# An encoder layer on one core: long attention tiles and the unit matrix at 32 bytes over a multiple of 128

## The chip, the core and the metric

The kernel runs on one core of a Trainium2 chip (trn2). The metric is the device time of one execution in microseconds: 2098.08 us in the median of 3 runs (2094.0 to 2100.1).

## What is computed

One post-norm layer over a sequence of 2048 rows of 1024 columns, float32, modulated by a conditioning vector. The input projection feeds two mixers. Mixer A takes trailing-window means over 2, 4, 8 and 16 frames in four channel groups. Mixer B is chunked attention with 8 heads of 64, in which each chunk of 64 rows looks at itself and the 8 chunks before.

```
mod = silu(c) @ w_ada + b_ada;  sh1, sc1, g1, sh2, sc2, g2 = split(mod)
h = x * (1 + sc1) + sh1
u, q, k, v = split(h @ w_in)
y_pool[g] = (window_sum(u[g], w[g]) / count - u[g]) @ w_pool[g] * pool_scale
y_attn = softmax(q @ k_band.T / 8 + bias, masked) @ v_band
x = layer_norm(2**0.25 * x + (1 + g1) * (concat(y_pool, y_attn) @ w_out))
h = x * (1 + sc2) + sh2
out = layer_norm(2**0.25 * x + (1 + g2) * (square(relu(h @ w_ff1)) @ w_ff2))
```

## The kernel before

All products of the projections are split: each float32 operand becomes a high part in fp32r and a low part (what is left), and three fp32r products (high by high, high by low, low by high) take the place of one float32 product. `split` (L58) makes the parts: ScalarE copies the high part, VectorE or GpSimd subtracts (L59, L60). The `Stream` (L62) loads weights into the two buffers `raw` and splits them into the three buffers `hl`.

The program is written in the order in which its engines run it; nothing is scheduled behind it (`manual_schedule`). It has four parts, one after the other:

1. The input projection with the attention beside it. `dense` (L421) goes through the heads and groups of output columns; each step issues 24 products of 128x512 (L446) into a PSUM bank, from the stationary weights `hl` and the moving rows `hT`. Between them the loop at the end of this part takes 128 units, each a block of 128 queries of one head: `scores` (L617) multiplies `q` by `k` (L628), VectorE adds the bias and takes the extreme value into the score tile `s` (L635), ScalarE exponentiates in place (L637), GpSimd divides in place (`normalise`, L640, at L643). Then `transposes` (L645) turns each 128x128 block of `s` on TensorE with the unit matrix `ident` as the moving operand (L651), `probs` splits it into `PT` (L659, L660), `values` multiplies by `v` (L672), and `combine` adds the halves into `y` through `yl` (L683, L684). The values `vt` are transposed with `ident` as well (L343).
2. The output projection (L407) and the first layer norm. The normalised rows `n` are transposed with `ident` (L844).
3. The first feed-forward product (L1070), in blocks of a 2 by 2 scheme with 7 products instead of 8.
4. The second feed-forward product (L1354), stationary `sa`, moving `sb`, and the second layer norm in `stats` and `ln2` (from L1314).

Mixer A is in `evac` (L316), in the branch from L350: `u` holds a halo of 16 columns that GpSimd copies from the block before, and 512 columns that ScalarE copies from PSUM; GpSimd then doubles the window in 1 to 4 sums between `ws0` and `ws1` (L361), VectorE subtracts (L370), and a DMA stores the result. `extras` (L498) sums the conditioning products in between, from tiles `xr` into `xa` (L514), and folds the pool weights `wp` into the output weights (L561).

Memory is given out by pools, in the order of the code. `const` and `small` hold what lives throughout, `stream` the buffers `raw` and `hl`; `ap` is the pool of the attention part, and the pools of the later parts take its place when it is closed. `padr` and `big` (the tiles `hT`, later `sb` and `g`) stand at the far end. Two fillers, `padr` (L118) and `pad` (L151), shift what follows them.

Of the kernel before, what the change touches and what calls it, by code (L numbers as in the profile page):

```python
# [8 lines left out]
F32 = mybir.dt.float32  # L9
F32R = mybir.dt.float32r  # L10
AF = mybir.ActivationFunctionType
ALU = mybir.AluOpType
# [12 lines left out]
def trunk_layer(ctx: ExitStack, tc: tile.TileContext, xT, x, wada1, wada2, vecs, rows, win, wfirst, wpT, wout,  # L25
# [2 lines left out]
    PS, DR = bass.MemoryType.PSUM, bass.MemoryType.DRAM  # L28
    ctx.enter_context(tc.manual_schedule())
    const = ctx.enter_context(tc.tile_pool(name="const", bufs=1))  # L30
    stream = ctx.enter_context(tc.tile_pool(name="stream", bufs=1))
    dram = ctx.enter_context(tc.tile_pool(name="scratch", bufs=1, space=DR))

    yS = [dram.tile([8, 128, 8, 128], F32, name=f"yS{i}") for i in range(2)]
# [8 lines left out]
    wS = [dram.tile([2, 128, 1024], F32, name=f"wS{i}") for i in range(16)]  # L43
    xS = [dram.tile([1024, 1024], F32, name=f"xS{i}") for i in range(2)]

    ident = const.tile([128, 128], F32, name="ident")
    make_identity(nc, ident)
    ones = const.tile([128, 1], F32, name="ones")
# [4 lines left out]
    nc.sync.dma_start(vec, vecs)  # L53
    mod1 = const.tile([128, 8, 2], F32, name="mod1")
    mods = const.tile([128, 2, 8], F32, name="mods")
    small = ctx.enter_context(tc.tile_pool(name="small", bufs=2))

    def split(hl_h, hl_l, src, low):  # L58
# [66 lines left out]


    e = small.tile([128, 8], F32, name="e")
    cs = const.tile([128, 8], F32, name="cs")
    nc.scalar.activation(e, vec[:, V_C:V_C + 8], AF.Exp, scale=-1.0)
    nc.vector.tensor_scalar(e, e, 1.0, None, op0=ALU.add)  # L130
    nc.vector.reciprocal(e, e)
# [184 lines left out]
    def evac(hf, kind, idx, tb, ps, bank):  # L316
        cols = slice(tb * 512, tb * 512 + 512)
        if kind == "A":
            q, kk = Qt[hf, idx], Kt[hf, idx]
            kc = slice(512 + tb * 512, 1024 + tb * 512)  # L320
            nc.scalar.activation(q[0:64, cols], ps[0:64], AF.Copy, scale=-0.125)
            nc.scalar.copy(kk[64:128, 0, kc], ps[64:128])
            yield
            nc.vector.scalar_tensor_tensor(q[64:128, cols], ps[0:64], -0.125, q[0:64, cols].bitcast(F32),
                                           op0=ALU.mult, op1=ALU.subtract)
            yield
            nc.vector.tensor_sub(kk[64:128, 1, kc], ps[64:128], kk[64:128, 0, kc].bitcast(F32))

            def copy():
                nc.sync.dma_start(kk[0:64, :, kc].bitcast(F32), kk[64:128, :, kc].bitcast(F32))  # L330
                if hf == 0 and tb == 1:
                    nc.sync.dma_start(kS[idx].bitcast(F32), kk[64:128, :, kc].bitcast(F32))

            after(12, copy)
        elif kind == "V":
            vv = Vt[hf, idx]
            vt = ap.tile([128, 512], F32, name="vt", bufs=1)
            nc.scalar.copy(vt, ps)  # L338
            for _ in range(9):
                yield  # L340
            pt = bank()
            for j in range(4):
                nc.tensor.transpose(pt[:, j * 128:j * 128 + 128], vt[:, j * 128:j * 128 + 128], ident)  # L343
            o = vv[:, 4 + tb * 4:8 + tb * 4]
            src = pt.rearrange("p (j h d) -> p j h d", j=4, h=2)
            nc.scalar.copy(o[:, :, :, 0:64], src)
            nc.vector.tensor_sub(o[:, :, :, 64:128], src, o[:, :, :, 0:64].bitcast(F32))
            if hf == 0 and tb == 1:
                after(12, lambda: nc.sync.dma_start(vS[idx].bitcast(F32), o.bitcast(F32)))
        else:  # L350
            wd = WINDOWS[idx]
            flush()
            u = ap.tile([128, 528], F32, name="u", bufs=1)
            nc.scalar.copy(u[:, 16:528], ps)
            nc.gpsimd.tensor_copy(u[:, 0:16], uh[:, idx, :])
            nc.gpsimd.tensor_copy(uh[:, idx, :], u[:, 512:528])
            ws = [ap.tile([128, 528], F32, name=f"ws{i}", bufs=1) for i in range(2)]
            cur, lo, sh, i = u, 0, 1, 0
            while sh < wd:
                lo += sh  # L360
                nc.gpsimd.tensor_add(ws[i][:, lo:528], cur[:, lo:528], cur[:, lo - sh:528 - sh])  # L361
                cur, i, sh = ws[i], 1 - i, 2 * sh
                for _ in range(3):
                    yield
            pl = ws[i][:, 16:528]
            for _ in range((30 if (hf, idx) == (0, 0) else 18) - 3 * (idx + 1)):
                yield
            if hf == 0 and tb == 0:
                nc.vector.tensor_mul(cur[:, 16:32], cur[:, 16:32], vec[:, V_CNT + 16 * idx:V_CNT + 16 * idx + 16])
            nc.vector.scalar_tensor_tensor(pl, cur[:, 16:528], 1.0 / wd, u[:, 16:528], op0=ALU.mult,  # L370
                                           op1=ALU.subtract)
            after(12, lambda: nc.sync.dma_start(
                yS[hf][tb * 4:tb * 4 + 4, :, idx, :].rearrange("t p c -> p t c"),
                pl.rearrange("p (t c) -> p t c", t=4)))
# [408 lines left out]

    load_x(0)
    load_x(1)
    a2 = const.tile([128, 8], F32, name="a2")
    b2 = const.tile([128, 8], F32, name="b2")
    nc.vector.tensor_mul(a2, vec[:, V_G:V_G + 8], mods[:, 1, :])
    nc.vector.tensor_mul(b2, vec[:, V_B:V_B + 8], mods[:, 1, :])
    nc.vector.tensor_add(b2, b2, mods[:, 0, :])  # L790
# [522 lines left out]

    def stats(t, halves=(0, 1)):  # L1314
        if t not in lns:
            lns[t] = (f2l.tile([128, 2, 6], F32, name="z6", bufs=5), f2l.tile([128, 4], F32, name="zv", bufs=5), [])
        s6, mv, got = lns[t]
        for i in halves:
            nc.vector.bn_stats(s6[:, i, :], acc[t][:, i * 512:i * 512 + 512])
# [149 lines left out]
```

## Time and profile before

| | |
|---|---|
| median of 3 runs | 2098.08 us |
| lowest and highest | 2094.0 and 2100.1 us |
| the profiled execution | 2097.0 us |
| its span, first to last instruction | 2095.3 us |
| granted TensorE clock, mean | 0.993 |
| TensorE busy with products | 2026.7 us, 97% |
| VectorE, ScalarE, GpSimd busy | 1311.3, 1000.4 and 323.1 us |
| moved by DMA | 456.68 MB, 218 GB/s |

Busy time is the time in which an engine works on an instruction; the weight loads of TensorE (PEld) overlap its products (PE). A matmul's own duration holds the way through the array, so that products that follow each other overlap in the rows: the pace of a series is the distance between the starts.

### The profile page before, as it was taken

The page shows a single profiled execution, that of the slowest core. Times are in us where ns is not written, and L with a number is a line of the kernel's source. Part 1 is how long each engine was busy: PE and PEld are TensorE (multiplying, and loading weights), DVE is VectorE, ACT ScalarE, POOL GpSimd, SP SyncE. Part 2 cuts the span into 40 slices and gives each one's busy share as a digit, 9 for nine tenths or more (in the row PEclk, how much of TensorE's full clock was granted, in tenths as well). Part 3 has the DMA queues.
Part 4 walks back from the last instruction along what each step waited for, and adds up shares of the span by engine and source line. Part 5 has one row for each costly group of instructions (what it writes and reads, how often), then busy time and mean ns, then how long its engine had stood idle before and what let it go on. Part 6 is the DMA issues. An engine that isn't in the chain of part 4 may idle for free.

```text
span 2095.3 us, 27047 instructions
## 1 busy us (share of the span) xinstructions
PE 2026.7 (97%) x9672; PEld 1682.5 (80%) x9672; DVE 1311.3 (63%) x1974; ACT 1000.4 (48%) x1592; POOL 323.1 (15%) x427
## 2 busy tenths in 40 slices
PE   7999989999999999899999999999999999999998
PEld 6788878887877888678888788888788888888886
DVE  7555566556665464777776766666594547875448
ACT  5544456555544545545555655545453333333330
POOL 1535443544233100000000000000000001000002
PEclk9999999999999999999999999999999999999999
DMA  7444543444443678879878988888886566776552
GB/s 299 137 136 135 144 148 103 132 119 141 130 128 100 190 252 285 297 262 321 289 275 300 313 281 307 295 295 284 318 290 219 190 199 211 248 239 234 193 171 110
DMA packets 210360, 456.68 MB, mean 218 GB/s; under 512 B 18609, under 2 KB 36529, under 8 KB 209202
## 3 DMA queue, kind: packets, MB, share of 16 engines
q1 hardware_dynamic: 210226, 454.96, 64.8%
q8 instruction: 76, 1.25, 0.3%
q14 instruction: 58, 0.48, 0.1%
HBM read 294.45 MB, written 152.05 MB: 213 GB/s over the span
## 4 chain that ended last, share of the span: by engine, by line
PE 80%; DVE 8%; ACT 4%; DMA 3%; issue 3%; POOL 1%; SPq 0%; DVEq 0%; POOLq 0%; ACTq 0%
PE f L1354 26%; PE f L1070 24%; PE d L446 11%; PE d L407 7%; PE pv L672 3%; PE T L651 3%; PE S L628 2%; DVE s L635 1%; ACT PT L659 1%; PE d L177 1%; DVE PT L660 1%; DMA raw<-in_w_dram 1%; PE S L177 1%; ACT s L637 1%; DVE sb L60 1%
## 5 line engine op out<-in xcount | busy, mean ns | idle before, releaser
L1354 PE MATMUL f<-sb,sa 128*128 128x512 f32 x2688 | 610.3, 389 | 2.7 <-DVE sb L60 1.9
L1354 PEld LDWEIGHTS f<-sb,sa 128*128 128x128 f32 x2688 | 504.4, 188 | 108.5 <-DVE sb L60 2.7
L446 PE MATMUL d<-hT,hl 128*128 128x512 f32 x1392 | 375.0, 401 | 0.7 <-ACT vt L338 0.7
L1070 PE MATMUL f<-h,hl 128*128 128x512 f32 x1536 | 361.3, 391 | 3.4 <-ACT c L1077 2.4
L1070 PEld LDWEIGHTS f<-h,hl 128*128 128x128 f32 x1536 | 288.8, 188 | 66.4 <-ACT c L1077 3.3
L1070 PE MATMUL f<-sb,hl 128*128 128x512 f32 x1152 | 275.5, 392 | 9.5 <-ACT c L1077 4.8
L446 PEld LDWEIGHTS d<-hT,hl 128*128 128x128 f32 x1392 | 250.0, 190 | 40.8 <-ACT vt L338 1.1
L1070 PEld LDWEIGHTS f<-sb,hl 128*128 128x128 f32 x1152 | 216.9, 189 | 58.4 <-ACT c L1077 6.0
L660 DVE TENSOR_TENSOR PT<-T,PT 128x640 fp32r<-128x640 f32 (+4 forms) x128 | 94.8, 741 | 210.4 <-ACT PT L659 208.3
L637 ACT ACTIVATE s<-s,m 128x640 f32<-128x640 f32 (+4 forms) x128 | 97.9, 764 | 237.9 <-DVE m L635 184.7
L407 PE MATMUL d<-hT,hl 128*128 128x512 f32 x696 | 165.3, 394 | 0.0
L1092 ACT ACTIVATE g<-g 128x512 f32<-128x512 f32 x96 | 60.7, 632 | 215.9 <-DVE g L1083 215.9
L59 ACT CAST sb<-hl 128x1024 fp32r<-128x1024 f32 x67 | 70.6, 1053 | 169.6 <-PE f L1354 140.9
L407 PEld LDWEIGHTS d<-hT,hl 128*128 128x128 f32 x696 | 129.6, 189 | 25.8
L643 POOL TENSOR_SCALAR s<-s,m 128x640 f32<-128x640 f32 (+4 forms) x128 | 99.1, 774 | 254.1 <-DVE m L642 213.3
L60 DVE TENSOR_TENSOR hl<-wsum,hl 128x1024 fp32r<-128x1024 f32 x64 | 78.4, 1225 | 93.7 <-ACT hl L59 93.6
L60 DVE TENSOR_TENSOR sb<-hl,sb 128x1024 fp32r<-128x1024 f32 x67 | 81.8, 1221 | 65.8 <-ACT sb L59 65.5
L59 ACT CAST sb<-raw 128x1024 fp32r<-128x1024 f32 x53 | 55.6, 1057 | 116.4 <-PE f L1354 83.0
L628 PE MATMUL S<-k,q 128*128 128x320 f32 (+1 forms) x448 | 92.6, 323 | 15.6 <-DVE m L635 15.6
L628 PEld LDWEIGHTS S<-k,q 128*128 128x128 f32 x448 | 74.9, 189 | 35.5 <-DVE m L635 21.6
L1397 POOL TENSOR_SCALAR ag<-ag 128x1024 f32<-128x1024 f32 x1 | 1.0, 1049 | 659.8 <-DMA ab<-in_rows_dram 659.8
L1323 POOL TENSOR_SCALAR zv<-zv 128x1 f32<-128x1 f32 x16 | 15.6, 974 | 549.2 <-DVE zv L1322 549.2
(183 smaller groups left out, 2658.6 us busy)
## 6 DMA issues: line engine op xcount, KB each, us to landing
fS<-g SPq DMA_DIRECT2D x224, 256.0 KB, 4.2
hl<-fS SPq DMA_DIRECT2D x67, 512.0 KB, 4.8
hl<-tS SPq DMA_DIRECT2D x67, 512.0 KB, 4.9
w<-in_w_dram SPq DMA_DIRECT2D x48, 512.0 KB, 4.3
raw<-fS SPq DMA_DIRECT2D x45, 512.0 KB, 4.7
raw<-tS SPq DMA_DIRECT2D x45, 512.0 KB, 4.7
wS<-wsum SPq DMA_DIRECT2D x32, 512.0 KB, 4.9
raw<-in_w_dram SPq DMA_DIRECT2D x32, 512.0 KB, 5.4
```

The source lines that it names most:

```text
L59: nc.scalar.copy(hl_h, src)
L60: low.tensor_sub(hl_l, src, hl_h.bitcast(F32))
L407: nc.tensor.matmul(ps, yc[:, a, k, :], hT(b, k, cols), start=(k == 0 and i == 0), stop=(k == 7 and i == 2))
L446: nc.tensor.matmul(ps, w[name][:, a, k, :], hT(b, k, slice(tb * 512, tb * 512 + 512)), start=(n == 0), stop=(n == 23))
L628: nc.tensor.matmul(S[:, 512 * p:512 * p + wp], q[:, i * 128:i * 128 + 128], k[:, a, k0 + p * wp:k0 + p * wp + wp], start=(a == 0), stop=(a ...
L637: nc.scalar.activation(s[:, 0:w], s[:, 0:w], AF.Exp, bias=m[:, 0:1], scale=-1.0, accum_out=m[:, 1:2])
L643: nc.gpsimd.tensor_scalar(s[:, 0:nk * 128], s[:, 0:nk * 128], m[:, 1:2], 1.0, op0=ALU.mult, op1=ALU.mult)
L651: nc.tensor.transpose(t[:, j * 128:j * 128 + 128], s[:, j * 128:j * 128 + 128], ident)
L660: nc.vector.tensor_sub(ol, src, oh.bitcast(F32))
L672: nc.tensor.matmul(pv, v[:, i + sl, h % 2, :], PTt[:, a, sl, :], start=(c == 0), stop=(c == tot - 1))
L1070: nc.tensor.matmul(ps, w[:, p, c:c + 128], h[:, q, k, :], start=first and k == 0 and (p, q) == (0, 0), stop=k == 3 and p == 1, skip_group_ ...
L1354: nc.tensor.matmul(bank, f, w, start=start, stop=stop, skip_group_check=True)
```

## The change

The change adds two small constants, `lead` at the start of the `const` pool and `fill` at its end, and moves `cs`, `a2`, `b2` and the opening of the `stream` pool, all of which sets places only. The tiles of the pooled rows get 544 columns instead of 528: the halo stands in columns 16 to 31 and the rows from column 32. In the second layer norm the two small tiles of `stats` are taken out of tiles of 32 columns. Places in a partition, in bytes over a multiple of 128, as the allocation of the two programs gives them:

| tiles | before | after |
|---|---|---|
| `ident`, `n` of the second layer norm | 0 | 32 |
| `ws0`, `s` (4 buffers), `xr` (8), `y`, `yl`, `xa`, `wp` | 96 | 32 |
| the rows behind the halo in `u` and `ws1`; in `ws0` | 96; 32 | 32 |
| `raw`, `hl`, `q`, `k`, `v`, `PT`, `bias`, `vt`, `u`, `ws1`, and the long tiles of parts 2 to 4 | 32 | 32 |
| `hT`, `sb`, `g` (far end) | 32 | 32 |

Counted over a multiple of 256, `ident` goes from 128 to 160, `s` and `xr` from 96 to 160, and `raw`, `hl`, `sa` and most others of the last row but one from 160 to 32; the tiles of the last row stay at 160.

```diff
-    stream = ctx.enter_context(tc.tile_pool(name="stream", bufs=1))
...
+    lead = const.tile([128, 8], F32, name="lead")
+    nc.vector.memset(lead, 0.0)
     ident = const.tile([128, 128], F32, name="ident")
...
+    cs = const.tile([128, 8], F32, name="cs")
+    a2 = const.tile([128, 8], F32, name="a2")
+    b2 = const.tile([128, 8], F32, name="b2")
+    fill = const.tile([128, 24], F32, name="fill")
+    nc.vector.memset(fill, 0.0)
+    stream = ctx.enter_context(tc.tile_pool(name="stream", bufs=1))
...
-            u = ap.tile([128, 528], F32, name="u", bufs=1)
-            nc.scalar.copy(u[:, 16:528], ps)
-            nc.gpsimd.tensor_copy(u[:, 0:16], uh[:, idx, :])
-            nc.gpsimd.tensor_copy(uh[:, idx, :], u[:, 512:528])
-            ws = [ap.tile([128, 528], F32, name=f"ws{i}", bufs=1) for i in range(2)]
-            cur, lo, sh, i = u, 0, 1, 0
+            u = ap.tile([128, 544], F32, name="u", bufs=1)
+            nc.scalar.copy(u[:, 32:544], ps)
+            nc.gpsimd.tensor_copy(u[:, 16:32], uh[:, idx, :])
+            nc.gpsimd.tensor_copy(uh[:, idx, :], u[:, 528:544])
+            ws = [ap.tile([128, 544], F32, name=f"ws{i}", bufs=1) for i in range(2)]
+            cur, lo, sh, i = u, 16, 1, 0
             while sh < wd:
                 lo += sh
-                nc.gpsimd.tensor_add(ws[i][:, lo:528], cur[:, lo:528], cur[:, lo - sh:528 - sh])
+                nc.gpsimd.tensor_add(ws[i][:, lo:544], cur[:, lo:544], cur[:, lo - sh:544 - sh])
...
-            pl = ws[i][:, 16:528]
+            pl = ws[i][:, 32:544]
...
-            nc.vector.scalar_tensor_tensor(pl, cur[:, 16:528], 1.0 / wd, u[:, 16:528], op0=ALU.mult,
+            nc.vector.scalar_tensor_tensor(pl, cur[:, 32:544], 1.0 / wd, u[:, 32:544], op0=ALU.mult,
...
-            lns[t] = (f2l.tile([128, 2, 6], F32, name="z6", bufs=5), f2l.tile([128, 4], F32, name="zv", bufs=5), [])
+            z6 = f2l.tile([128, 32], F32, name="z6", bufs=5)[:, 0:12].rearrange("p (i c) -> p i c", i=2)
+            lns[t] = (z6, f2l.tile([128, 32], F32, name="zv", bufs=5)[:, 0:4], [])
```

The engines' lists of instructions differ in one place. On VectorE at the program's start, where `e` and `cs` are the conditioning vector's activation and `wa` the first of its weights, the list before is:

```order
1 L49 MEMSET ones 128x1
2 L130 TENSOR_SCALAR e<-e 128x8
3 L131 RECIPROCAL e<-e 128x8
4 L132 TENSOR_TENSOR cs<-e,vec 128x8
5 L134 TENSOR_SCALAR vec<-vec 128x8
6 L188 TENSOR_SCALAR ac<-wa,cs 128x256 x2
```

and with the change, whose line numbers are 2 to 7 higher:

```order
1 L47 MEMSET lead 128x8
2 L51 MEMSET ones 128x1
3 L62 MEMSET fill 128x24
4 L137 TENSOR_SCALAR e<-e 128x8
5 L138 RECIPROCAL e<-e 128x8
6 L139 TENSOR_TENSOR cs<-e,vec 128x8
7 L141 TENSOR_SCALAR vec<-vec 128x8
8 L195 TENSOR_SCALAR ac<-wa,cs 128x256 x2
```

Two memsets stand around the one that was there; everything behind them, and every other engine's list, is in the order it had.

## Rows read from the trace of the kernel before

**Rows 1.** Stretches: us and busy us (instructions) of each engine, clock, DMA share, GB/s.

```profile
90.00:650.00 560.00, 535.79 (x3029) 454.55 (x3028) 328.76 (x728) 296.22 (x603) 245.36 (x296) 0.99 0.45 130
1460.00:2096.00 636.00, 622.93 (x2745) 514.63 (x2743) 405.25 (x409) 236.02 (x235) 31.43 (x34) 0.99 0.64 219
```

**Rows 2.** The chain that ended last, from the page: shares of the span.

```profile
PE 80%; DVE 8%; ACT 4%; DMA 3%; issue 3%; POOL 1%; SPq 0%; DVEq 0%; POOLq 0%; ACTq 0%
```

**Rows 3.** Who TensorE waited for, 90 to 650 us: us, times, longest.

```profile
PE S L628 <- DVE m L635: 13.2, 11, 2.9
PE T L651 <- DVE PT L660: 8.9, 13, 2.4
PEld S L628 <- DVE m L635: 18.4, 13, 3.4
```

**Rows 4.** Transposes: groups (busy, mean ns), then timeline (start, us).

```profile
L651 PE MATMUL T<-ident,s 128*128 128x128 f32 x560 | 83.4, 275 | 11.8 <-DVE PT L660 10.3 <-POOL hl L60 1.1
L343 PE MATMUL d<-ident,vt 128*128 128x128 f32 x64 | 9.7, 274 | 1.4 <-ACT vt L338 1.1 <-ACT u L354 0.3
L844 PE MATMUL T<-ident,n 128*128 128x128 f32 x72 | 9.4, 273 | 1.1 <-ACT n L801 1.1
L844 PE MATMUL S<-ident,n 128*128 128x128 f32 x56 | 7.2, 272 | 0.0
...
403.10 0.71 PE L651 MATMUL T<-ident,s 128*128 128x128 f32 x5
...
759.99 1.03 PE L844 MATMUL T<-ident,n 128*128 128x128 f32 x8
```

**Rows 5.** Float32 products from tiles at 96, timeline.

```profile
173.72 1.02 PE L525 MATMUL d<-xa,square 128*128 128x512 f32 x2
...
182.74 1.02 PE L561 MATMUL d<-xr,wp 128*128 128x512 f32 x2
```

**Rows 6.** fp32r products, timeline: in the attention, in the second feed-forward product.

```profile
401.70 1.56 PE L446 MATMUL d<-hT,hl 128*128 128x512 f32 x6
...
1489.78 550.51 PE L1354 MATMUL f<-sb,sa 128*128 128x512 f32 x2428
```

**Rows 7.** ScalarE's groups by shape: the exponential (96), the cast into PT (32).

```profile
L637 ACT ACTIVATE s<-s,m 128x640 f32<-128x640 f32 x96 | 79.8, 831 | 191.3 <-DVE m L635 159.7 <-DVE m L642 31.3
L637 ACT ACTIVATE s<-s,m 128x128 f32<-128x128 f32 x8 | 3.2, 403 | 8.7 <-DVE m L642 4.7 <-DVE m L635 4.0
L659 ACT CAST PT<-T 128x640 fp32r<-128x640 f32 x96 | 66.0, 688 | 27.4 <-PE pv L672 17.4 <-PE T L651 8.3
L659 ACT CAST PT<-T 128x128 fp32r<-128x128 f32 x8 | 2.1, 264 | 3.7 <-PE pv L672 2.5 <-PE T L651 1.2
```

**Rows 8.** VectorE's groups by shape: tiles at 96, 32, 0 and 32.

```profile
L635 DVE CUSTOM_DVE_ANT_0 s<-S,bias 128x640 f32<-128x640 f32 x96 | 78.4, 817 | 4.9 <-PE S L628 4.1
L660 DVE TENSOR_TENSOR PT<-T,PT 128x640 fp32r<-128x640 f32 x96 | 79.1, 824 | 163.1 <-ACT PT L659 163.0
L1335 DVE SCALAR_TENSOR_TENSOR n<-n,zv,r 128x1024 f32<-128x1024 f32 x12 | 15.4, 1285 | 5.9 <-POOL zv L1324 5.4
L1129 DVE SCALAR_TENSOR_TENSOR tw<-raw,cs,tw 128x1024 f32<-128x1024 f32 x7 | 9.0, 1284 | 2.1 <-DMA raw<-in_wada_dram 2.1
```

**Rows 9.** GpSimd by line (min/median/max ns): tiles at 96, tiles at 32.

```profile
L555 POOL TENSOR_TENSOR xr<-xr,xa x8: 1283/1292/1300, 253.3 to 435.1; 128x512 f32<-128x512 f32 x8
...
L60 POOL TENSOR_TENSOR hl<-raw,hl x58: 1272/1292/2275, 46.6 to 577.5; 128x512 fp32r<-128x512 f32 x58
```

**Rows 10.** DMA queue (packets, MB, share): 613:617, xr<-woS alone; 1598:1602, raw<-fS alone.

```profile
q1 hardware_dynamic: 147, 0.27, 19.9%
...
q1 hardware_dynamic: 273, 0.52, 35.6%
```

**Rows 11.** VectorE's start, timeline.

```profile
0.79 0.06 DVE L49 MEMSET ones<- 128x1 f32 x1 [0.79 <-PEq L1462]
2.81 0.17 DVE L130 TENSOR_SCALAR e<-e 128x8 f32<-128x8 f32 x1 [1.96 <-ACT e L129]
```

More of the change, by code (lines that the diff above doesn't have):

```diff
@@ L127, in trunk_layer @@
     e = small.tile([128, 8], F32, name="e")
-    cs = const.tile([128, 8], F32, name="cs")
     nc.scalar.activation(e, vec[:, V_C:V_C + 8], AF.Exp, scale=-1.0)
@@ L368, in evac @@
             if hf == 0 and tb == 0:
-                nc.vector.tensor_mul(cur[:, 16:32], cur[:, 16:32], vec[:, V_CNT + 16 * idx:V_CNT + 16 * idx + 16])
-            nc.vector.scalar_tensor_tensor(pl, cur[:, 16:528], 1.0 / wd, u[:, 16:528], op0=ALU.mult,
+                nc.vector.tensor_mul(cur[:, 32:48], cur[:, 32:48], vec[:, V_CNT + 16 * idx:V_CNT + 16 * idx + 16])
+            nc.vector.scalar_tensor_tensor(pl, cur[:, 32:544], 1.0 / wd, u[:, 32:544], op0=ALU.mult,
                                            op1=ALU.subtract)
@@ L785, in trunk_layer @@
     load_x(1)
-    a2 = const.tile([128, 8], F32, name="a2")
-    b2 = const.tile([128, 8], F32, name="b2")
     nc.vector.tensor_mul(a2, vec[:, V_G:V_G + 8], mods[:, 1, :])
```

## The prediction

> **What bounds the kernel now.** I read the stretches first, then the chain of waits, then who waited in the attention, then single instructions whose tiles stand at different places. [...] The chain [rows 2] is 80% PE. So a change of places in memory can alter the time in two ways only: a TensorE instruction that reads a moved tile gets another pace, or another engine's instruction gets another duration and one of TensorE's waits goes with it. The second way has little room: in the attention TensorE is idle for 560 - 535.8 = 24.2 us in all, most of it in front of the scores and the transposes, until VectorE is done [rows 3].
>
> **The change part by part.** No instruction is moved, none is dropped, and no wait gets another partner: in the built programs each engine's list differs by two VectorE memsets alone. What is left is the places, and each is priced below from instructions that already stand at the place to which others go.
>
> *The transposes.* 752 transposes read the unit matrix as the moving operand, and it goes from 0 to 32 over a multiple of 128. They are 560 of the probabilities, 64 of the values and 72 + 56 of the normalised rows [rows 4]. The tile that is transposed stands at 96 for the probabilities and at 32 for the other two, and that makes no difference: five probability blocks in 0.71 us, the last of them 0.275 long, give a pitch of (0.71 - 0.275) / 4 = 109 ns, and eight blocks of rows in 1.03 us give (1.03 - 0.27) / 7 = 108.6 ns. So moving the probabilities from 96 to 32 is priced at nothing. A moving float32 operand at 32 has no row next to one at 0, so I bound it. The nearest rows are the plain float32 products that stream 512 columns from a tile at 96, which like 32 is not a multiple of 64 [rows 5]: two of them in 1.02 us, one 0.59 long, so 0.43 us for 512 columns or 107.5 ns for 128. Against 109 ns at 0 that leaves a gain of 1.5 ns on 752, or 1.1 us. The other end: 2428 fp32r products, whose moving operand stands at 32, take 550.51 us, so 226.7 ns for 512 columns [rows 6], and half of the float32 product's 430 ns is 215. If the 11.7 ns between them were a charge for standing at 32 that each instruction pays once, 752 transposes would lose 8.8 us. I take 0, since it is the plain float32 product at 96 that is nearest to a transpose, and it streams at the pace of the transposes.
>
> *The elementwise work on score tiles (96 to 32).* ScalarE's exponential, in place at 96, grows by 831 - 403 = 428 ns from 128 to 640 columns; its cast into the transposed tile, which stands at 32 already, grows by 688 - 264 = 424 [rows 7]. VectorE writes the scores at 96 in 817 ns and subtracts into the tile at 32 in 824 ns, both 640 columns; the normalised rows, now at 0, take 1285 ns and the same operation on a tile at 32 takes 1284 [rows 8]. GpSimd's product of two tiles at 96 has a median of 1292 ns, and its subtraction of two tiles at 32 has 1292 too [rows 9]. The price is therefore nothing at 0, 32 and 96 alike, so no wait of TensorE is moved. The bound in the other direction is 1%: 4 ns in 428, which on a score chain of three such operations is about 25 ns in each of 128 units, 3 us if all of it were waited for, and less than that since the 13.2 and 18.4 us of waiting [rows 3] come from 11 and 13 units.
>
> *Pooled rows in 544 columns.* The number of elements in each copy, sum and product stays (the sums still cover 527, 525, 521 and 513). The two sources of each sum keep their distance, 1, 2, 4 or 8 elements, and only the distance from the sources to the target changes. They are on GpSimd and have many microseconds before their result is needed, as GpSimd is busy for 245 of 560 us in that stretch [rows 1]. Price nothing; their cover is that the stores of pooled rows are read only by the output projection.
>
> *The DMAs.* Transfers into and out of the tiles at 96 now use tiles at 32, and every other tile allocated behind the constants, such as the stream's, moves by 128 bytes, which leaves its place over 128 as it was. In stretches with one transfer, 2 KB rows into a tile at 96 take 19.9% of 16 engines over 4 us, 12.7 us for 128 rows or 99 ns a row; into a tile at 32 they take 35.6%, 22.8 us for 256 rows or 89 ns [rows 10]. I take no change, because the attention moves 130 GB/s at a DMA share of 0.45 [rows 1] and nothing there waits for longer transfers. If it were 10 ns a row for address alone, it would be given back inside that idle share.
>
> [...]
>
> *Two memsets* on VectorE at the start, 8 and 24 columns. One memset there takes 0.06 us, and behind it VectorE waits 1.96 us for ScalarE [rows 11], so both are covered; without that cover they would cost 0.12 us.
>
> **The sum.** 0 + 0 + 0 + 0 + 0 against the profiled execution's 2097.0 us (span 2095.3). That execution stands 1.1 us below the median of the runs shown, 2098.1, and I forecast the median: **2098 us**.
>
> **The rivals.**
> *The unit matrix at 32 costs the transposes something* (slower). Place: the moving read of 752 transposes on TensorE, which nothing covers in the attention. Price: the upper bound above, 8.8 us, so 2107. It decides from 6.3 us / 752 = 8.4 ns per transpose, a pitch of 117 instead of 109. Against it: the float32 products from tiles at 96 [rows 5]. Chance 0.05.
> *The distance between the two operands of a product matters.* In the second feed-forward product the stationary tile moves by 128 bytes and the moving one, at the far end of the memory, does not. Every fp32r product now has both at the same place over 256, so no row excludes this in either direction. Price: six such products of the attention take 1.56 us, (1.56 - 0.40) / 5 = 232 ns, against 226.7 in the long row [rows 6]; the 5.3 ns between the two paces on 2428 products are 13 us, so 2085 or 2111. Against it: the transposes, whose pairs stand at 0 with 96 and at 0 with 32, have one pace [rows 4]. Chance 0.06, half on each side.
> *The moved score tiles are quicker* and TensorE's waits shrink. If a third of the 24.2 us went, 8 us, it would be 2090. Against it: equal durations at three places [rows 7 to 9]. Chance 0.06.
> *The transfers of all moved tiles get shorter.* If each 2 KB row lost the 10 in 99 ns that separate the two tiles of rows 10, the 3% of the chain that are transfers [rows 2], some 63 us, would lose 6.4 us: 2092, at the edge of 0.3%. Against it: the dearer tile's rows come from a transfer half as long, in which the first rows weigh more. Chance 0.05, put to no change. [...]
> *The change does not do what it says*: excluded for the places, which the allocation shows; the tiles that matter most for TensorE stood at 32 before, and that is the reason for the forecast.
>
> **How the numbers follow.** 0.3% is 6.3 us, about what a measurement of this kernel can tell from no change; the three runs shown lie 6.1 us apart. Forecast 0.78, transfers 0.05: same 0.83 less 0.01 for a median that strays, 0.82. Faster: 0.06 + 0.03, and 0.01 for straying, 0.10. Slower: 0.05 + 0.03 = 0.08. The range takes the runs' own spread, 2094.0 to 2100.1, and reaches down from 2098 by the 8 us of the third rival, and up by the 8.8 us of the first: 2090 to 2107. Left out are the second rival and a stray median.
>
> **What would show it.** Right: transposes still at 109 ns, the long row of second feed-forward products still at 226.7 ns, the exponential at 831 ns, the attention's idle time near 24 us. Wrong: another pace in either of those TensorE rows (the first or second rival), or score operations shorter by more than 10 ns and TensorE's idle time in the attention below 18 us (the third).

## The result and the profile after

The changed kernel took **2122.78 us** in the median of 5 runs (2121.49 to 2128.88), against 2098.08 for the kernel before; the ratio is 1.0125 (95% interval 1.011 to 1.014). Forecast were 2098 us, 2090 to 2107, and a chance of 0.08 for slower: the forecast is wrong by 24.7 us, and its range misses too.

First the page of the changed kernel, its line of busy times:

```profile
PE 2051.8 (97%) x9672; PEld 1685.0 (79%) x9672; DVE 1313.9 (62%) x1976; ACT 1000.1 (47%) x1592; POOL 323.3 (15%) x427
```

TensorE works on its products for 2051.8 us where it was 2026.7. That is 25.1 us more, and the span has grown by 24.4 (2119.7 for 2095.3). The other engines' busy times have moved by less than 3 us. So the lost time is in the products themselves. The groups of TensorE by shape, with busy us and mean ns of one, say in which:

```profile
L1360 PE MATMUL f<-sb,sa 128*128 128x512 f32 x2688 | 625.6, 395 | 2.7 <-DVE sb L68 1.7 <-ACT sb L67 1.0
L453 PE MATMUL d<-hT,hl 128*128 128x512 f32 x1392 | 376.2, 403 | 0.7 <-ACT vt L345 0.7
L1075 PE MATMUL f<-h,hl 128*128 128x512 f32 x1536 | 361.0, 390 | 2.7 <-ACT c L1082 2.0 <-DVE h L68 0.7
L1075 PE MATMUL f<-sb,hl 128*128 128x512 f32 x1152 | 281.6, 397 | 9.5 <-ACT c L1082 5.0 <-DVE g L1088 2.5 <-ACT sb L67 1.2
L414 PE MATMUL d<-hT,hl 128*128 128x512 f32 x696 | 167.7, 397 | 0.0
...
L658 PE MATMUL T<-ident,s 128*128 128x128 f32 x560 | 83.3, 275 | 12.1 <-DVE PT L667 10.7 <-POOL hl L68 1.1
```

Before, the same groups by shape read 610.3 us and 389 ns (second feed-forward, now L1360), 375.0 and 401 (L453), 361.3 and 391 (`f<-h,hl`), 275.5 and 392 (`f<-sb,hl`), 165.3 and 394 (L414). The growth is 15.3 + 1.2 - 0.3 + 6.1 + 2.4 = 24.7 us. The two lines of L1075 are the telling pair. Before, as L1070, they read:

```profile
L1070 PE MATMUL f<-h,hl 128*128 128x512 f32 x1536 | 361.3, 391 | 3.4 <-ACT c L1077 2.4 <-DVE h L60 0.9
L1070 PE MATMUL f<-sb,hl 128*128 128x512 f32 x1152 | 275.5, 392 | 9.5 <-ACT c L1077 4.8 <-DVE g L1083 3.6 <-DVE sb L60 0.8
```

It is one line of code, with the same stationary tiles `hl`. The products whose moving tile is `h`, near the stream, cost what they did; those whose moving tile is `sb`, at the far end, cost 5.3 ns more each. In the one group both operands were moved by 128 bytes, in the other only one. The transposes have not changed (83.4 us and 275 ns before, [rows 4]).

The stretches show the attention untouched and the second feed-forward product slower. The columns are those of [rows 1]:

```profile
90.00:650.00 560.00, 536.47 (x3035) 454.70 (x3033) 328.98 (x728) 296.23 (x603) 245.50 (x296) 0.99 0.44 131
...
1460.00:2096.00 636.00, 633.30 (x2724) 513.36 (x2724) 393.96 (x388) 240.19 (x242) 24.94 (x26) 1.00 0.64 218
```

The granted clock is 0.99 and 1.00, where both stretches had 0.99 before, so it is not the clock. In the last stretch the trace has 21 fewer TensorE instructions for 10 us more of work. The timeline shows the pace; its first line is five transposes of the attention, and its last is the long row of second feed-forward products that follow each other:

```profile
403.85 0.71 PE L658 MATMUL T<-ident,s 128*128 128x128 f32 x5
...
1496.50 583.77 PE L1360 MATMUL f<-sb,sa 128*128 128x512 f32 x2511 [0.76 <-DVE sb L68]
```

Five transposes take 0.71 us as in [rows 4]. The long row goes at 583.77 / 2511 = 232.5 ns a product from start to start (one record is 395 ns long), against 550.51 / 2428 = 226.7 in [rows 6]. What TensorE waits for in the attention stayed too (compare [rows 3]):

```profile
PE S L635 <- DVE m L642: 13.0, 11, 2.9
```

and so did the elementwise work on the score tiles, 832 ns for 831 on ScalarE [rows 7] and 817 for 817 on VectorE [rows 8]:

```profile
L644 ACT ACTIVATE s<-s,m 128x640 f32<-128x640 f32 x96 | 79.9, 832 | 191.2 <-DVE m L642 159.7 <-DVE m L649 31.4
...
L642 DVE CUSTOM_DVE_ANT_0 s<-S,bias 128x640 f32<-128x640 f32 x96 | 78.4, 817 | 4.8 <-PE S L635 3.7 <-POOL hl L68 0.4
```

### The profile page after: what moved, and what is told of

It reads as the page before. It is cut to its first block, busy times and chain, and to the rows that moved or that the text cites. A ratio compares the mean times of both kernels' runs of the same rounds, so it can differ in the third digit from the quotient of the medians.

```text
span 2119.7 us, 27049 instructions
## 1 busy us (share of the span) xinstructions
PE 2051.8 (97%) x9672; PEld 1685.0 (79%) x9672; DVE 1313.9 (62%) x1976; ACT 1000.1 (47%) x1592; POOL 323.3 (15%) x427
## 3 DMA queue, kind: packets, MB, share of 16 engines
q1 hardware_dynamic: 210226, 454.96, 63.9%
## 4 chain that ended last, share of the span: by engine, by line
PE 82%; DVE 7%; ACT 4%; DMA 3%; issue 3%; POOL 1%; SPq 0%; DVEq 0%; POOLq 0%; ACTq 0%
PE f L1360 27%; PE f L1075 26%; PE d L453 11%; PE d L414 7%; PE pv L679 3%; PE T L658 2%; PE S L635 2%; DVE s L642 1%; DMA raw<-in_wada_dram 1%; ACT PT L666 1%; PE d L184 1%; DVE PT L667 1%; PE S L184 1%; ACT s L644 1%; PE S L414 1%
## 5 line engine op out<-in xcount | busy, mean ns | idle before, releaser
L1360 PE MATMUL f<-sb,sa 128*128 128x512 f32 x2688 | 625.6, 395 | 2.7 <-DVE sb L68 1.7
L1360 PEld LDWEIGHTS f<-sb,sa 128*128 128x128 f32 x2688 | 506.9, 189 | 121.3 <-DVE sb L68 2.5
L453 PE MATMUL d<-hT,hl 128*128 128x512 f32 x1392 | 376.2, 403 | 0.7 <-ACT vt L345 0.7
L1075 PE MATMUL f<-h,hl 128*128 128x512 f32 x1536 | 361.0, 390 | 2.7 <-ACT c L1082 2.0
L1075 PEld LDWEIGHTS f<-h,hl 128*128 128x128 f32 x1536 | 288.2, 188 | 67.1 <-ACT c L1082 2.8
L1075 PE MATMUL f<-sb,hl 128*128 128x512 f32 x1152 | 281.6, 397 | 9.5 <-ACT c L1082 5.0
L453 PEld LDWEIGHTS d<-hT,hl 128*128 128x128 f32 x1392 | 250.6, 191 | 40.8 <-ACT vt L345 1.1
L1075 PEld LDWEIGHTS f<-sb,hl 128*128 128x128 f32 x1152 | 216.8, 189 | 63.3 <-ACT c L1082 6.1
L414 PE MATMUL d<-hT,hl 128*128 128x512 f32 x696 | 167.7, 397 | 0.0
L414 PEld LDWEIGHTS d<-hT,hl 128*128 128x128 f32 x696 | 129.5, 189 | 28.2
L650 POOL TENSOR_SCALAR s<-s,m 128x640 f32<-128x640 f32 (+4 forms) x128 | 99.0, 774 | 254.3 <-DVE m L649 215.6
```

The source lines that it names most:

```text
L414: nc.tensor.matmul(ps, yc[:, a, k, :], hT(b, k, cols), start=(k == 0 and i == 0), stop=(k == 7 and i == 2))
L453: nc.tensor.matmul(ps, w[name][:, a, k, :], hT(b, k, slice(tb * 512, tb * 512 + 512)), start=(n == 0), stop=(n == 23))
L650: nc.gpsimd.tensor_scalar(s[:, 0:nk * 128], s[:, 0:nk * 128], m[:, 1:2], 1.0, op0=ALU.mult, op1=ALU.mult)
L1075: nc.tensor.matmul(ps, w[:, p, c:c + 128], h[:, q, k, :], start=first and k == 0 and (p, q) == (0, 0), stop=k == 3 and p == 1, skip_group_ ...
L1360: nc.tensor.matmul(bank, f, w, start=start, stop=stop, skip_group_check=True)
```

## The experiments: whole kernels

**The theories.** *Distance*: an fp32r product takes longer when its moving and its stationary tile do not stand at the same place over 256 bytes. *Place*: it is the place of one tile that counts, the near tiles being worse at 32 over 256 than at 160. *Moved set*: the slower part is something the change moves on purpose (unit matrix, score tiles, pooled rows). Below, d is the place of the moving tile less that of the stationary one, in bytes over a multiple of 256, for the second feed-forward product. It was 0 before and is 128 after, and it is the same for the other products that read the far end. In the expectation of e5_before_far256 the far end's tiles are called stationary by mistake; `sb` and `hT` there are the moving ones.

**The far end follows, or goes alone.** In the first kernel the changed one gets a larger filler, so that the far end too moves down by 128 bytes; in the second the kernel before gets the same filler and nothing else of the change.

```diff
-    nc.gpsimd.memset(padr.tile([128, 16], F32, name="padr"), 0.0)
+    nc.gpsimd.memset(padr.tile([128, 48], F32, name="padr"), 0.0)
```

> The changed kernel with the far end (hT, sb, g) moved down by 128 bytes too, so that a product's two operands stand at the same place over 256 again. Distance theory (a product is slower when its stationary and moving tile differ by 128 over 256): second feed-forward pace back from 232.8 to 226.7 ns, mean duration back from 395 to 389 ns, time 2095 to 2101 us. Place theory (the near tiles are slower at their new place, whatever they meet): stays at 395 ns and 2120 to 2126 us. Moved-set theory (ident, s, n, ws at 32 are to blame): stays at 2120 to 2126 us.

> The kernel before with nothing but the far end moved down by 128 bytes. Distance theory: products with one operand at the far end slow down as in the change (mean duration 395 instead of 389 ns in the second feed-forward product), 2119 to 2126 us. Place theory and moved-set theory: no near tile moves, so 2094 to 2101 us.

The first took 2098.84 us, 1.0005 of the kernel before (0.9993 to 1.0017); the second 2122.25, 1.0121 (1.0101 to 1.0142). Their long rows in the timeline, first of e1, then of e2:

```profile
1489.73 600.01 PE L1360 MATMUL f<-sb,sa 128*128 128x512 f32 x2639 [0.77 <-DVE sb L68]
```

```profile
1493.61 606.78 PE L1354 MATMUL f<-sb,sa 128*128 128x512 f32 x2610 [0.76 <-DVE sb L60]
```

That is 227.4 and 232.5 ns. The whole change with d back at 0 is as quick as the kernel before, and a filler of 128 bytes alone is as slow as the whole change. So everything that the change does on purpose is, taken together, worth nothing in time to within the first one's interval, and the moved set falls as a cause.

**The near tiles move by a whole 256.** The changed kernel with a larger `fill`: the near tiles stand 256 bytes above where they were in the kernel before, so d is 0 again, with the near tiles at 160 over 256.

```diff
-    fill = const.tile([128, 24], F32, name="fill")
+    fill = const.tile([128, 56], F32, name="fill")
```

> The changed kernel with its second filler 128 bytes longer, so that the near tiles stand 256 bytes past their place of before and ident, s and the others keep 32 over 128. Distance theory with a period of 256: 2095 to 2101 us and 389 ns. Distance theory with a period of 512 or more: slower than before, 395 ns or another value, 2105 to 2126 us. Moved-set theory: 2120 to 2126 us.

2097.92 us, 1.0006 (0.9996 to 1.0015), and in the long row 600.09 / 2639 = 227.4 ns:

```profile
1487.09 600.09 PE L1360 MATMUL f<-sb,sa 128*128 128x512 f32 x2639 [0.76 <-DVE sb L68]
```

With e1, where near and far stand at 32 over 256, and e3, where both stand at 160, place falls too: the quick kernels have the near tiles at either, the slow e2 has them where the kernel before has them. The pair also bears on the transfers. The stream tiles are at 32 over 256 in e1 and at 160 in e3, and the two ratios differ by 0.0001 with intervals of 0.001 to each side: the place of the stream tiles is not seen in this kernel's time. In the transfers themselves it is worth little: the queue's packets took 63.8% of 2100.4 us in e1 and 64.1% of 2097.9 us in e3, 0.4% more, and 63.9% of 2119.7 us with the change, at 32, against 64.8% of 2095.3 us before, at 160, 0.2% less.

**Other distances.** The kernel before with `padr` of other widths. Each 8 columns more put the far end 32 bytes lower; a far end that is k bytes lower has d = 256 - k.

```diff
-    nc.gpsimd.memset(padr.tile([128, 16], F32, name="padr"), 0.0)
+    nc.gpsimd.memset(padr.tile([128, 32], F32, name="padr"), 0.0)
```

That is the one with 64 bytes; for 32, 96, 192, 224 and 256 the width is 24, 40, 64, 72 and 80.

> The kernel before with the far end moved down by 64 bytes: stationary and moving tile 64 apart over 128. Distance theory: if only equality over 256 is fast, the second feed-forward product takes 395 ns in the mean again or worse, 2115 us or more; if the cost grows with the distance up to 128, about half of it, 2105 to 2115 us. Place and moved-set theory: 2094 to 2101 us.

> The kernel before with the far end 256 bytes lower (stationary tiles of both feed-forward products and hT), so that stationary and moving tile of every fp32r product again stand at the same place over 256. Distance theory with a period of 256: as before, ratio 1.000 (0.998 to 1.002), the group f<-sb,sa at 389 to 390 ns mean and 610 to 612 us. Rival, the distance itself counts and not its remainder (any shift of the far end costs): 2121 to 2125, as with 64 and 128.

> The kernel before with the far end 32 bytes lower. If any distance other than none over 256 costs the same: 2121 to 2125, f<-sb,sa at 625 to 628 us. If the cost grows with the distance: about 2104, a quarter of what 128 bytes cost. If it is 64-byte lines that must coincide: as before, 2098.

> The kernel before with the far end 192 bytes lower, which over 256 is 64 higher. If only being at the same place counts: 2121 to 2125. If the direction counts (which of the two tiles runs ahead over 256), this one differs from the one with 64 bytes lower: between 2090 and 2115, and 2098 if that direction costs nothing.

> The kernel before with the far end 96 bytes lower. If any distance other than none over 256 costs the same: 2121 to 2125. If some distance is quicker than none: below 2090, with the steady pitch of the second feed-forward products under 226 ns; I have no row that points to one.

> The kernel before with the far end 224 bytes lower, so that the moving tiles stand 32 bytes further over 256 than the stationary ones. From the first bench (233.5 ns at d = 32 against 226.7 at 0, about 6.8 ns) on 4536 products: 31 us, 2127, between 2121 and 2130. If only one direction of the distance costs, as the runs with 64 lower (1.0134) and 192 lower (1.0065) could be read: 2098 to 2110.

The last was run after the first bench below and forecast from it. The long rows, in the order e4, e5, e6, e7, e8, e11:

```profile
1501.93 598.30 PE L1354 MATMUL f<-sb,sa 128*128 128x512 f32 x2563 [0.76 <-DVE sb L60]
```

```profile
1483.84 598.48 PE L1354 MATMUL f<-sb,sa 128*128 128x512 f32 x2639 [0.76 <-DVE sb L60]
```

```profile
1500.12 600.16 PE L1354 MATMUL f<-sb,sa 128*128 128x512 f32 x2571 [0.77 <-DVE sb L60]
```

```profile
1492.71 604.32 PE L1354 MATMUL f<-sb,sa 128*128 128x512 f32 x2639 [0.76 <-DVE sb L60]
```

```profile
1499.69 600.49 PE L1354 MATMUL f<-sb,sa 128*128 128x512 f32 x2562 [0.76 <-DVE sb L60]
```

```profile
1501.47 598.76 PE L1354 MATMUL f<-sb,sa 128*128 128x512 f32 x2565 [0.77 <-DVE sb L60]
```

| kernel | d | median us | ratio (95% interval) | long row, ns a product |
|---|---|---|---|---|
| e5, far end 256 lower | 0 | 2096.86 | 1.0004 (0.9994 to 1.0013) | 226.8 |
| e11, 224 lower | 32 | 2129.0 | 1.0158 (1.0141 to 1.0175) | 233.4 |
| e7, 192 lower | 64 | 2109.34 | 1.0065 (1.0048 to 1.0082) | 229.0 |
| e2, 128 lower | 128 | 2122.25 | 1.0121 (1.0101 to 1.0142) | 232.5 |
| e8, 96 lower | 160 | 2129.7 | 1.0161 (1.0145 to 1.0176) | 234.4 |
| e4, 64 lower | 192 | 2125.0 | 1.0134 (1.0117 to 1.0151) | 233.4 |
| e6, 32 lower | 224 | 2124.82 | 1.0135 (1.0119 to 1.0152) | 233.4 |

The period of 256 holds (e5: 226.8 ns, 1.0004). Of the three readings that e6 was to tell apart, "any distance costs about the same" is the nearest, though e8 came out above the 2121 to 2125 that it gave; the cost does not grow with the distance (233.4 ns in e6 at 32 lower, 232.5 in e2 at 128 lower), and 64-byte lines are not it (2124.82 us in e6, where they gave 2098). e7 shows that the sign counts: 64 further costs half of 64 back (1.0065 and 1.0134). No distance is quicker than 0, and so no version that beats the kernel before came out of this.

## The experiments: the products by themselves

**A first bench.** Behind the last product of the kernel before, groups of 32 products whose results nobody reads, each group on its own line of code, from the last stationary and the last moving tile of the second feed-forward product. The first column of the moving or of the stationary operand is shifted:

```diff
+    for n in range(32): nc.tensor.matmul(XB[0][:, :512], pf[:, 0 + 128 * (n % 8):128 + 128 * (n % 8)], pw[:, 0 + 512 * (n % 4):512 + 512 * (n % 4)], **mm(n))
+    for n in range(32): nc.tensor.matmul(XB[0][:, :512], pf[:, 0 + 128 * (n % 8):128 + 128 * (n % 8)], pw[:, 4 + 512 * (n % 4):516 + 512 * (n % 4)], **mm(n))
...
```

> The kernel before, and behind its last product a bench of products whose results nobody reads: groups of 32 back to back from the last stationary tile and the last moving tile of the second feed-forward product, the moving operand d bytes further over 256 than the stationary one, d = 0, 16, 32 to 240. If the runs with a shifted far end were read rightly, the pace of a group of 512 columns is 227 ns at d = 0, about 230 at 64, 233 at 128, 234 at 160, 233 at 192 and 224, and the groups with both operands 64 bytes up are at 227 again, since the distance counts and not the place. If the pace in those runs came from something else that the far end's shift brings (a bank of the memory, other tiles' traffic), all groups here have one pace. If the charge is paid once per product (the load of its 128 stationary columns), 256 and 128 columns at d = 192 lose the same 5 to 6 ns; if it is paid per column, 3 and 1.5 ns. [...] bf16 (d = 0, 32, 64, 128, 192, 224): I expect a difference there too if the two reads meet in the memory, none if it is the format's. It is some 250 us longer than before.

The timeline of the bench (start us, us). L1421 is d = 0 and each line after it 16 bytes more, up to 240 in L1436; L1437 is d = 0 again. L1441 and L1442 have 256 columns at d = 0 and 192, L1447 and L1448 are plain float32 at d = 0 and 192, L1453 and L1454 are bf16 at d = 0 and 32:

```profile
2094.09 7.42 PE L1421 MATMUL f<-sb,sa 128*128 128x512 f32 x32
2101.34 7.58 PE L1422 MATMUL f<-sb,sa 128*128 128x512 f32 x32
2108.76 7.63 PE L1423 MATMUL f<-sb,sa 128*128 128x512 f32 x32
2116.23 7.62 PE L1424 MATMUL f<-sb,sa 128*128 128x512 f32 x32
2123.69 7.50 PE L1425 MATMUL f<-sb,sa 128*128 128x512 f32 x32
2131.02 7.56 PE L1426 MATMUL f<-sb,sa 128*128 128x512 f32 x32
...
2153.28 7.62 PE L1429 MATMUL f<-sb,sa 128*128 128x512 f32 x32
2160.75 7.62 PE L1430 MATMUL f<-sb,sa 128*128 128x512 f32 x32
...
2183.16 7.62 PE L1433 MATMUL f<-sb,sa 128*128 128x512 f32 x32
2190.62 7.67 PE L1434 MATMUL f<-sb,sa 128*128 128x512 f32 x32
2198.14 7.62 PE L1435 MATMUL f<-sb,sa 128*128 128x512 f32 x32
2205.59 7.42 PE L1436 MATMUL f<-sb,sa 128*128 128x512 f32 x32
2212.85 7.45 PE L1437 MATMUL f<-sb,sa 128*128 128x512 f32 x32
...
2242.35 4.00 PE L1441 MATMUL f<-sb,sa 128*128 128x256 f32 x32
2246.18 3.81 PE L1442 MATMUL f<-sb,sa 128*128 128x256 f32 x32
2249.83 3.69 PE L1443 MATMUL f<-sb,sa 128*128 128x128 f32 x32
...
2256.93 27.68 PE L1447 MATMUL f<-sb,sa 128*128 128x512 f32 x64
2284.44 27.63 PE L1448 MATMUL f<-sb,sa 128*128 128x512 f32 x64
...
2350.48 7.07 PE L1453 MATMUL f<-sb,sa 128*128 128x512 bf16 x32
2357.39 7.07 PE L1454 MATMUL f<-sb,sa 128*128 128x512 bf16 x32
```

The pace of a group is the distance to the next group's start over 32. At d = 0 it is (2101.34 - 2094.09) / 32 = 226.6 ns, at 16 it is 231.9, at 32 it is 233.4, at 64 it is 229.1, at 128 it is 233.4, at 192 it is 233.1, at 224 it is 232.8 and at 240 it is 226.9. Times the 2688 + 1152 + 696 = 4536 products that grew, d = 64 is worth 2.5 x 4536 = 11 us, d = 128 is worth 31 and d = 192 is worth 29. The whole kernels lost 13.6, 25.4 and 28.1 (ratio less one, times 2097). So the bench gives the size of the loss to some 5 us, and it does so with nothing but the two addresses changed. It does not give the order of 128 and 192. At d = 128 the same addresses took 231.9 ns in the second bench below (L1426 there), which would make 24 us.

The formats differ. Plain float32 takes 27.51 / 64 = 429.8 ns a record at d = 0, with two records to a product, and bf16 6.91 / 32 = 215.9 at d = 0; all the other distances tried gave the same to 1 ns (float32 429.2 at 192 and a group as long, 27.63 us, at 64; bf16 215.6 to 215.9 from 32 to 192, and at 224 a group of 7.07 us like the others). (L1452, a first bf16 group at d = 0, is left out: it stands behind 2.58 us of waiting and took 8.52 us, and from 2342.0 to 2345.2 us the granted clock was 0.52.) Here the expectation for bf16 missed. The one for 256 columns missed as well: they are dearest at d = 0, 3.83 / 32 = 119.7 ns, and take 114.1 at 192; 128 columns take 110.0 and 111.9. So the charge is neither a fixed sum per product nor a share per column.

**How a series settles.** L1437 is d = 0 once more, and it took 227.8 ns where L1421 took 226.6. The difference lies in its first products. The next two lines are its last 23 products, from a timeline that begins at 2215.12 us, and the first product of the group behind it:

```profile
2214.93 5.38 PE L1437 MATMUL f<-sb,sa 128*128 128x512 f32 x23
2220.14 0.39 PE L1438 MATMUL f<-sb,sa 128*128 128x512 f32 x1
```

The first nine products start (2214.93 - 2212.85) / 9 = 231 ns apart, the other 23 start (2220.14 - 2214.93) / 23 = 226.5 apart. So a series at d = 0 can need several products before it runs at the quick pace. This fits the attention. Its products of L446 stand in series of at most nine, most of them of five or six, and in the kernel before the distance between two starts falls from 233.5 ns behind the first of a series to 228.1 behind the sixth, in the mean; with the change these are 232.6 and 235.9. The mean over all of them is 231.8 before and 232.5 after. Series that end before they settle have little to lose by d = 128, and this group grew by 1.2 us only.

**A second bench.** What meets what: pairs that agree while the next product's stationary tile stands elsewhere, and the other way round, from sources of this form:

```diff
+    for n in range(32): nc.tensor.matmul(XB[0], S(n, 32 * (n % 2)), M(n, 32 * (n % 2)), **mm(n))
+    for n in range(32): nc.tensor.matmul(XB[0], S(n, 32 * (n % 2)), M(n, 32 - 32 * (n % 2)), **mm(n))
...
```

> A second bench behind the kernel before, groups of 32 fp32r products of 128 stationary by 512 moving columns. What meets: if a product's own two operands must stand at one place over 256, the group whose pairs agree but whose next stationary tile stands 128 bytes off stays at 227 ns, and the group whose pairs differ by 128 while the next stationary tile agrees goes to 233. If it is the stationary tile of the next product, read while the current one's columns stream, that meets the moving one, the two groups come out the other way round: 233 and 227. With one and the same stationary tile for every product at d = 192: 233 if the address counts and not the change. Fewer stationary columns (64, 32) at d = 192: a smaller charge, towards 227, if the charge is the meeting of two reads; the same 6 ns if it is paid once per product. Steps of 4 and 8 bytes: a mix between 227 and 231. 384 columns: a charge of 4 to 6 ns at d = 32 to 192 if as with 512; 256 columns: the sign turned, as in the first bench, 120 ns at d = 0 and 114 at 192.

L1424: pairs agree, the next stationary tile stands 128 off. L1425: pairs 128 apart, the next agrees. L1426: 128 in both. L1427: pairs agree, the next is 32 off. L1452 and L1453: one stationary tile throughout, at d = 0 and 192.

```profile
2097.26 7.48 PE L1424 MATMUL f<-sb,sa 128*128 128x512 f32 x32
2104.58 7.52 PE L1425 MATMUL f<-sb,sa 128*128 128x512 f32 x32
2111.94 7.59 PE L1426 MATMUL f<-sb,sa 128*128 128x512 f32 x32
2119.36 7.58 PE L1427 MATMUL f<-sb,sa 128*128 128x512 f32 x32
2126.78 7.57 PE L1428 MATMUL f<-sb,sa 128*128 128x512 f32 x32
...
2272.41 7.42 PE L1452 MATMUL f<-sb,sa 128*128 128x512 f32 x32
2279.66 7.63 PE L1453 MATMUL f<-sb,sa 128*128 128x512 f32 x32
2287.13 7.63 PE L1454 MATMUL f<-sb,sa 128*128 128x512 f32 x32
```

The paces are 228.8, 230.0, 231.9 and 231.9 ns, where either simple picture wanted 227 in one of the first two and 233 in the other. Both relations seem to count in part, and the run does not decide between them. With one stationary tile throughout, d = 192 still costs 233.4 against 226.6, so the change of address from product to product is not it. With 64 stationary columns these two distances lie closer together (230.0 at d = 0 and 232.8 at 192), and with 32 they are equal (231.6 and 231.9); all of these are dearer than 128 columns at d = 0. The third bench shows that this is no smaller charge yet. Two expectations missed: steps of 4 and 8 bytes took 230.0 to 237.8 ns instead of 227 to 231, and 384 columns, expected 4 to 6 ns dearer, lost nothing at d = 32 and 64.

**A third bench.** The first run under this name held the second bench's code by mistake. It took 2297.36 us, where the second bench took 2297.46, and came out within 0.3 ns of the second bench in every group, so a group repeats as long as the same groups stand before it. Behind other groups the same addresses differ by up to 2 ns (d = 128 took 233.4 in the first bench and 231.9 in the second), so smaller differences between benches are not read as an effect of the addresses. Its expectation:

> A third bench behind the kernel before, groups of 32 fp32r products of 512 columns, both operands moved together by 8 to 224 bytes. In the second bench both moved by 16 bytes went to 233 ns and both by 128 stayed at 227.5. If the place counts besides the distance only below 32 bytes, both moved by 32, 64, 96, 128, 160, 192 and 224 stay at 227 to 228 and 8, 16, 24, 40 and 48 are dear; if only multiples of 64 are free, 32, 96, 160 and 224 are dear too, which the kernels with both sets 128 bytes up or down cannot tell. At a base moved by 32 or 128, d = 32, 64 and 192 cost as at the base: 233, 229 and 233. If the charge is a matter of how the two reads fall in time, 64 stationary columns have another favourable distance than 0: some d among 16, 32, 64, 128, 224, 240 under 229, where d = 0 took 230.1.

Then the bench itself, in which both operands move together:

```diff
+    for n in range(32): nc.tensor.matmul(XB[0], S(n, 4), M(n, 4), **mm(n))
+    for n in range(32): nc.tensor.matmul(XB[0], S(n, 6), M(n, 6), **mm(n))
+    for n in range(32): nc.tensor.matmul(XB[0], S(n, 8), M(n, 8), **mm(n))
...
```

> The third bench itself (the kernel sent as e12_probe3 was by mistake the second bench again), groups of 32 fp32r products of 512 columns, both operands moved together by 8 to 224 bytes from their place at 160 over 256. In the second bench both moved by 16 bytes went to 233 ns and both by 128 stayed at 227.5. If the place counts besides the distance only below 32 bytes, both moved by 32, 64, 96, 128, 160, 192 and 224 stay at 227 to 228 and 8, 16, 24, 40 and 48 are dear; if only multiples of 64 are free, 32, 96, 160 and 224 are dear too, which the kernels with both sets 128 bytes up or down cannot tell. At a base moved by 32 or 128, d = 32, 64 and 192 cost as at the base: 233, 229 and 233. With 64 stationary columns some d among 16, 32, 64, 128, 224, 240 under 229 if another distance suits them, where d = 0 took 230.1.

L1425, L1426 and L1427 have both operands 16, 24 and 32 bytes up:

```profile
2105.20 7.55 PE L1425 MATMUL f<-sb,sa 128*128 128x512 f32 x32
2112.60 7.73 PE L1426 MATMUL f<-sb,sa 128*128 128x512 f32 x32
2120.16 7.44 PE L1427 MATMUL f<-sb,sa 128*128 128x512 f32 x32
2127.44 7.61 PE L1428 MATMUL f<-sb,sa 128*128 128x512 f32 x32
```

231.3, 236.3 and 227.5 ns. Both moved by 64, 96, 128, 160, 192 or 224 gave 227.5 to 228.1. At a base 32 and at one 128 bytes up, d = 32, 64 and 192 cost 233, 229 and 233 as at the first base. So for tiles at multiples of 32 bytes the distance over 256 alone sets the pace of these products, to 1.5 ns; between multiples of 32 the common place counts as well. There the second bench had 233.4 ns with both 16 bytes up where this one has 231.3, so what ran before has some part in it. With 64 stationary columns another distance suits better (227.5 at 16 bytes, 230.0 at 0, 233.1 at 240): from the best to the worst it is 5.6 ns, hardly less than with 128 columns.

## Why the prediction was wrong

**The step that failed** is the rival "The distance between the two operands of a product matters" as it was weighed and sized, and with it the part on the change, which had no term for the fp32r products. The mechanism is what happened, on its slow side: the long row went from 226.7 to 232.5 ns a product, and the three groups with a far moving tile and longer series lost 15.3 + 6.1 + 2.4 = 23.8 us where the sum had nothing.

- *Its chance.* It got 0.03 on the slow side, although the prediction itself said that "no row excludes this in either direction". What spoke against it was the one pace of the transposes at two distances. The bench shows why that was no evidence: the transposes are plain float32, and plain float32 has one pace at every distance tried (429.8 ns a record at 0, 429.2 at 192). Over 256 the 560 transposes of the probabilities stood at d = 128 - 96 = 32 before and stand at 0 now, and they kept their pace (five in 0.71 us both times). (The bench also corrects the reading of [rows 5]: two records there are one product, not two.)
- *Its size.* The price per product was nearly right, 5.3 ns against 232.5 - 226.7 = 5.8. But it was put on the 2428 products of one row alone, 13 us. The same pair, far moving tile and near stationary tile, is in all 2688 products of that line, in 1152 of the first feed-forward and in 696 of the output projection: at 5.3 ns, 4536 of them make 24 us and 2122. That count is made with the result in hand: counted beforehand, the attention's 1392 have the same pair, which makes 31 us and 2129. This rival's 2111 stood outside the range already, since the range left it out on purpose.
- *The reason for the forecast*, that "the tiles that matter most for TensorE stood at 32 before", counted places over 128, each tile by itself. What decides is the difference of two tiles over 256, which went from 0 to 128. The table of the change had those numbers.
- *Where that price came from.* The 232 ns of six products in the attention was not a distance: these pairs stood at d = 0 when it was read, and the 1392 products of that line grew by 1.2 us only. It was the pace of series that end before they settle. That it came near the price of d = 128 is luck.

**What held.** The transposes cost nothing (275 ns each, 0.71 us for five); neither did the score tiles (832 for 831 ns, 817 for 817), the pooled rows, the transfers or the two memsets: e1, which has all of the change but d = 128, is at 1.0005. TensorE's idle time in the attention is 560 - 536.47 = 23.5 us for 24.2. Together these terms of the sum were right at 0, to the interval of e1, -1.5 to +3.6 us; the pooled rows and the transfers were not measured one by one. So the rivals on the unit matrix, the score tiles and the transfers fall.

**What is not settled** is what in the hardware makes the pace depend on the distance. With 128 stationary and 512 moving columns it belongs to fp32r among the three formats tried (226.6 ns at d = 0 and 233.1 at 192, two distances at which float32 and bf16 differ by less than 1 ns), and it needs no change of the stationary tile (233.4 at d = 192 against 226.6 at 0 with one tile throughout). Two reads that meet in the memory are the author's guess at it, which no run shows. The runs with fewer stationary columns do not decide it. Why a series takes several products to settle is not known either.

## What to carry to other kernels

Before a filler moves some tiles, list for every long series of fp32r products of 512 columns where its stationary and its moving tile stand over 256 bytes, and keep the two at the same place, at multiples of 32: here 128 bytes of filler cost 1.2%, and one of 32 bytes 1.35%. For other widths this is no rule: 256 columns were dearest at the same place (119.7 ns, and 114.1 at d = 192). Price a mechanism that no row excludes on every group that it reaches, not on the row in which it was noticed. And an operation in one format is no evidence for another: the transposes' even pace (275 ns each at d = 32 and at 0) said nothing on the products.

## What the runs showed of the hardware that was not expected

- The pace of fp32r products with 512 moving and 128 stationary columns ran from 226.6 to 238 ns with addresses alone, the dearest with the moving operand 4 bytes further or 12 bytes behind (237.2 and 237.8 in the second bench). So the time of these products depends on how their two addresses stand to each other.
- A series at d = 0 is not always quick from its first product: behind other groups L1437 of the first bench needed nine, and the attention's short series, between other products, kept to 231.8 ns in the mean.
- At d = 0, 512, 384 and 256 columns take 226.6, 173.4 and 120.0 ns in the second bench. The differences are 53.2 and 53.4 ns for 128 columns, 0.416 ns a column, and 4 x 53.3 = 213.2 leave 13.4 ns for each product of 512. The bf16 products of 512 columns take 215.9 ns in the first bench, 2.7 more than 213.2; how their time grows with the columns was not measured.
- The favourable distance depends on the width: 384 columns are as quick at d = 32 and 64 as at 0 (173.4 at 32, 173.1 at 64) and dearest of those tried at 240 (179.7), where 512 were as quick as at 0 (226.9 and 226.6); 256 columns are dearest at 0 (120.0, the other distances 114.4 to 118.4; all in the second bench, but for 512 at 240).
